# A decoder trunk on one core: down's weights on GpSimd's queue, another cut of the seven-product groups, another opening and a shorter final norm

## The chip, the cores and the metric

The kernel runs on one NeuronCore of a Trainium2 chip. The core has TensorE (PE, matrix products; its weight loads are listed apart as PEld), VectorE (DVE), ScalarE (ACT), GpSimd (POOL) and SyncE (SP), which run side by side and wait for one another through semaphores. Data comes from HBM by DMA; a DMA is issued in order on the queue of one engine, and all queues are served by the same 16 DMA engines. The metric is the device time of one execution in microseconds (us). Time before: 1836.87 us, the median of three runs (1836.17 to 1838.67).

## The reference

The input x is 512 tokens by 1024 features in float32. Two layers follow one another; layer 0 has a gated linear attention (GLA) as its mixer and layer 1 a stick-breaking attention (SB). Each layer is

```
x = x + 0.5 * swiglu(rmsnorm(x, ffn1_norm[i]), gate, up, down)
h = rmsnorm(x, mix_norm[i]);  x = x + mixer_i(h)
x = x + 0.5 * swiglu(rmsnorm(x, ffn2_norm[i]), gate, up, down)
```

with `swiglu(h) = (silu(h @ w_gate) * (h @ w_up)) @ w_down`, `rmsnorm(x, g) = x * rsqrt(mean(x*x) + 1e-6) * g`, w_gate and w_up of 1024 x 2816 and w_down of 2816 x 1024. A final rmsnorm with `final_norm` gives the output. The four FFNs hold most of the arithmetic, and the change is in them, in the first microseconds ahead of them and in the final norm.

## The kernel before

**Arithmetic.** Every product is float32 by three passes. A matrix a is cut in two fp32r parts: ScalarE casts it (h, line L126), VectorE subtracts (l = a - h, L127), and TensorE adds h·h, l·h and h·l. The two lines stand in `Entry.split`; the tiles are wh and wl, four buffers of each. The activations are kept the same way (xh/xl, nh/nl, th/tl, hh/hl) with features on the 128 partitions and the 512 tokens along the free dimension.

**The feed.** All weight work is a list of entries in `Feed`. An entry has units (a chunk of weights in HBM, a view of it, its size) and a body, which issues the products. When entry i starts, `Feed.start` (L142) looks ahead: it cuts the next entries' units, as far as the four wh/wl buffers go, builds the views (sums) of the next four, and issues the loads of the next six. `Chunk.load` (L91) issues a load on SyncE's queue, into the tag raw (gate, up, mixers: 1 MB, two buffers) or the tag rawd (down: 512 KB, two buffers of their own). A load waits on the queue until its buffer is free, and what stands behind it waits too. Each queue and each engine works strictly in order.

**Seven-product groups.** Most gate and up weights, and a part of down's, are multiplied by a Strassen-Winograd scheme: a tile is seen as four quarters A11, A12, A21, A22, and seven products of quarter size replace eight. For gate and up this is `FFN.seven` (L665 to L771): two entries per group. The first has as units A11 together with A12 (one cut of 128 x 1024, name ax) and the sums s12 (L677, L678 on VectorE); its four products go to the PSUM tiles ps_w, ps_q, ps_w and ps_z, and ScalarE copies ps_w to ps_z (L718) after the first. The second has the sums s34 (L683, L684) and A22 (128 x 512), with three products; L704 and L707 then apply silu or the gate and put the result together. A product is 12 matmuls (L694) of 128 x 256. For down it is `seven_down` (L333 to L427): the same scheme on two rawd chunks (lower and upper), with sums at L353 to L361, matmuls at L369, additions to x at L375, and the two copies of ps_w to ps_z at L387, which TensorE needs before it writes ps_w again in the third product. Down's other groups are plain (`down`, addition at L324). Within an FFN of six groups, the second and the fourth group's down is by seven products.

**The opening** (`begin`, L1495 to L1690) is written out by hand and pinned in order: loads of x and of the first gate (eg) and up (eu) weights in halves (L1527), 32 transposes of x (`turn`, L1574), scaling into xh and xl (`scale`), cuts of the first weights (L1544, L1546), 48 products (L1599) in the order gate 0-1, transposes, gate 2-3, up 0-1, transposes, up 2-3, the norm's factor R (L1665), and 24 products more. The feed's own products follow (L66).

**The end** (`to_tokens`, L1441; `last`, L1458). The last FFN's down products give tokens by features. fin, the final norm's gains on all partitions, is loaded on GpSimd's queue (L1445). For each of four token tiles: x is added up (L1462), ScalarE squares it with a sum (L1471), `rstd_1` (L494) turns the two sums into the factor r in six steps on VectorE and ScalarE (an addition, a square root, a reciprocal, and three steps that refine it), x and xf are scaled (L1478, L1480), and both leave on SyncE's queue (L1479, L1481). The last tile's second half comes in two pieces of 256 columns.

## Time and profile before

| what | value |
|---|---|
| median of three runs | 1836.87 us |
| profiled execution | 1839.01 us |
| its span, first to last instruction | 1837.2 us |
| mean granted TensorE clock | 0.998 |
| TensorE busy | 1821.0 us (99%), 12476 matmuls |
| VectorE busy | 1530.1 us (83%) |
| ScalarE busy | 1068.4 us (58%) |
| GpSimd busy | 8.7 us, 20 instructions |
| DMA by SyncE's queue | 176.18 MB, 30.2% of the 16 engines' time |
| DMA by GpSimd's queue | 1.05 MB |
| last output issued | 1833.91 us |

The profile is of one execution. Starts are microseconds from its first instruction. A row of a timeline gives start, duration, engine, line, operation and tiles, and in brackets how long the engine had been idle before it and what released it. A row of the waits gives who waited for whom, the total, how many times, and the longest. The granted clock is that of TensorE as a share of full speed. PEld overlaps PE. A queue is written as SPq, ACTq or POOLq.

### The profile page before, as it was taken

Reading aid. Unit: us, or ns where it says so; the run is one execution under the profiler, and the core shown is the slowest. Engines: PE = TensorE matmul, PEld = TensorE weight load, DVE = VectorE, ACT = ScalarE, POOL = GpSimd, SP = SyncE. Lnnn points to the kernel's source line nnn. Section 1 sums busy time; section 2 is a strip of 40 time slices with the busy share of each in tenths; the row PEclk is TensorE's granted clock in tenths of the full one; section 3 lists DMA queues with packets and bytes.
Section 4 is the critical chain, followed back from the end, with each engine's and each line's share of the span. In section 5 each row is a group of like instructions: output and inputs, shape, how many; then the busy total and the mean of one; then the engine's idle time right before and its main releaser. Section 6 shows DMA issues by size and latency. Waiting matters only on the chain. (4 is left out here: it accounts for less than half of the span.)

```text
span 1837.2 us, 30777 instructions
## 1 busy us (share of the span) xinstructions
PE 1821.0 (99%) x12476; PEld 1657.2 (90%) x12476; DVE 1530.1 (83%) x2509; ACT 1068.4 (58%) x1842; POOL 8.7 (0%) x20
## 2 busy tenths in 40 slices
PE   8999999999999999999999999999999999999998
PEld 7999999889888899999889999998888788999997
DVE  8999797776787989888798988976878769898885
ACT  6556565444555556555565555645878855565554
POOL 0000000100000000000000000000000000000000
PEclk9999999999999999999999999999999999999999
DMA  5333324221223232323233232322221222333331
GB/s 161 118 124 116 103 93 139 79 69 49 68 69 115 92 111 97 127 93 115 75 121 107 91 125 92 119 86 85 70 70 58 69 92 92 115 106 113 104 104 69
DMA packets 177649, 179.20 MB, mean 98 GB/s; under 512 B 4130, under 2 KB 168020, under 8 KB 177508
## 3 DMA queue, kind: packets, MB, share of 16 engines
q1 hardware_dynamic: 176800, 176.18, 30.2%
q8 instruction: 97, 1.59, 0.4%
q0 software_dynamic: 608, 1.05, 0.2%
q14 instruction: 44, 0.36, 0.1%
q10 hardware_dynamic: 100, 0.03, 0.0%
HBM read 175.17 MB, written 2.10 MB: 96 GB/s over the span
## 5 line engine op out<-in xcount | busy, mean ns | idle before, releaser
L127 DVE TENSOR_TENSOR wl<-raw,wh 128x1024 fp32r<-128x1024 f32 x242 | 256.0, 1061 | 88.0 <-ACT wh L126 46.6
L126 ACT CAST wh<-raw 128x1024 fp32r<-128x1024 f32 (+1 forms) x242 | 223.0, 922 | 157.4 <-PE ps_f L66 35.7
L127 DVE TENSOR_TENSOR wl<-s,wh 128x1024 fp32r<-128x1024 f32 x176 | 214.0, 1219 | 40.4 <-PE ps_z L694 38.5
L694 PE MATMUL ps_w<-th,wh 128*128 128x256 f32 x864 | 239.0, 277 | 0.3
L694 PE MATMUL ps_w<-tl,wh 128*128 128x256 f32 x864 | 238.7, 276 | 0.0
L694 PE MATMUL ps_w<-th,wl 128*128 128x256 f32 x864 | 238.7, 276 | 0.0
L126 ACT CAST wh<-s 128x1024 fp32r<-128x1024 f32 x176 | 184.9, 1050 | 82.8 <-DVE s L684 27.7
L66 PE MATMUL ps_f<-xh,wh 128*128 128x512 f32 x432 | 172.5, 399 | 0.0
L66 PE MATMUL ps_f<-xl,wh 128*128 128x512 f32 x432 | 169.3, 392 | 0.0
L66 PE MATMUL ps_f<-xh,wl 128*128 128x512 f32 x432 | 168.9, 391 | 0.0
L694 PEld LDWEIGHTS ps_w<-th,wh 128*128 128x128 f32 x864 | 162.2, 188 | 0.9 <-ACT ps_z L718 0.9
L694 PEld LDWEIGHTS ps_w<-th,wl 128*128 128x128 f32 x864 | 162.4, 188 | 0.0
L66 PE MATMUL ps_d<-hh,wl 128*128 128x512 f32 x416 | 162.2, 390 | 0.0
L66 PE MATMUL ps_d<-hh,wh 128*128 128x512 f32 x416 | 162.2, 390 | 0.0
L694 PEld LDWEIGHTS ps_w<-tl,wh 128*128 128x128 f32 x864 | 162.2, 188 | 0.0
L66 PE MATMUL ps_d<-hl,wh 128*128 128x512 f32 x416 | 161.8, 389 | 0.0
L126 ACT CAST wh<-rawd 128x1024 fp32r<-128x1024 f32 (+1 forms) x84 | 81.5, 971 | 96.7 <-PE ps_d L66 45.0
L127 DVE TENSOR_TENSOR wl<-rawd,wh 128x1024 fp32r<-128x1024 f32 (+1 forms) x84 | 93.2, 1118 | 20.7 <-PE ps_z L694 11.5
L324 DVE SCALAR_TENSOR_TENSOR x<-ps_d,x 128x512 f32<-128x512 f32 x120 | 80.9, 686 | 21.4 <-PE ps_d L66 21.0
L66 PEld LDWEIGHTS ps_f<-xl,wh 128*128 128x128 f32 x432 | 81.1, 188 | 17.3
L66 PEld LDWEIGHTS ps_f<-xh,wl 128*128 128x128 f32 x432 | 81.3, 188 | 15.6
L66 PEld LDWEIGHTS ps_f<-xh,wh 128*128 128x128 f32 x432 | 81.3, 188 | 15.4
(348 smaller groups left out, 5279.8 us busy)
## 6 DMA issues: line engine op xcount, KB each, us to landing
raw<-in_ffn_w_gate_dram SPq DMA_DIRECT2D x43, 1024.0 KB, 5.3
raw<-in_ffn_w_up_dram SPq DMA_DIRECT2D x43, 1024.0 KB, 5.7
rawd<-in_ffn_w_down_dram SPq DMA_DIRECT2D x84, 512.0 KB, 3.6
raw<-in_gla_w_in_dram SPq DMA_DIRECT2D x12, 1024.0 KB, 5.4
raw<-in_sb_w_in_dram SPq DMA_DIRECT2D x16, 512.0 KB, 3.8
raw<-in_gla_w_out_dram SPq DMA_DIRECT2D x4, 1024.0 KB, 5.0
raw<-in_sb_w_in_dram SPq DMA_DIRECT2D x4, 1024.0 KB, 5.2
raw<-in_sb_w_out_dram SPq DMA_DIRECT2D x4, 1024.0 KB, 5.0
```

Of the source, the lines that this page charges most:

```text
L66: st["pe"] = nc.tensor.matmul(ps, l, r, start=first, stop=last).ins
L126: st["cut"] = nc.scalar.copy(h, r).ins
L127: nc.vector.tensor_tensor(out=l, in0=r, in1=h.bitcast(F32), op=ALU.subtract)
L324: nc.vector.scalar_tensor_tensor(out=xs[k], in0=ps, scalar=0.5, in1=xs[k], op0=ALU.mult, op1=ALU.add)
L694: st["pe"] = nc.tensor.matmul(o, l_, r_, start=first and j + n == 0, stop=j == 3 and n == 2, skip_group_check=True).ins
```

## The change

**Loads.** A chunk of down's weights is loaded through GpSimd's queue instead of SyncE's. The buffers stay as they are, two of tag rawd.

**Seven-product groups.** The first entry of a group has three units: A11 alone (512 columns), the sums s12, and a2, which is A12 together with A22 (1024). The second entry has only s34; its last product takes A22 from a2. `Entry.split` can cut a unit that comes in two pieces, since down's A12 and A22 lie in two tiles: such a unit is two casts and two subtractions of 512. For gate and up the number and sizes of the cuts are the same as before; for down, 16 cuts of 1024 columns become 32 of 512. The products themselves and their order are the same.

**Opening.** The up weights' first half is loaded before the second half of x. Ten matmuls of the ones tile by itself, 128 columns each, whose result is overwritten, are put among the first transposes (six ahead, one each before the third and the fourth tile's, two behind). The first 24 products, gate 0-3 and up 0-3, follow one another, and all 16 transposes of the second half of x come behind them; the scalings and cuts on ScalarE and VectorE are reordered to suit.

**Final norm.** fin is scaled once by a constant on VectorE. `rstd_1` adds the second sum inside the square root's instruction, and refines with one division less: r = 1/(y + v/y). In the last tile the last square is taken on VectorE, x is scaled and sent in two halves of 256 columns, and xf leaves on ScalarE's queue.

The diff, cut to its core:

```diff
@@ -88,7 +88,7 @@
                     self.t = st["few"].tile([P, self.n, self.m], F32, tag="rawd", bufs=2, name="rawd")
                 else:
                     self.t = wp.tile([P, self.n, self.m], F32, tag="raw", bufs=2, name="raw")
-                nc.sync.dma_start(self.t, self.src)
+                (nc.gpsimd if self.few else nc.sync).dma_start(self.t, self.src)
...
-                    st["cut"] = nc.scalar.copy(h, r).ins
-                    nc.vector.tensor_tensor(out=l, in0=r, in1=h.bitcast(F32), op=ALU.subtract)
+                    pieces = r if isinstance(r, tuple) else (r,)
+                    for i, part in enumerate(pieces):
+                        k = slice(i * n // len(pieces), (i + 1) * n // len(pieces))
+                        st["cut"] = nc.scalar.copy(h[:, k], part).ins
+                        nc.vector.tensor_tensor(out=l[:, k], in0=part, in1=h[:, k].bitcast(F32), op=ALU.subtract)
...
-        feed.q.append(
-            Entry([(lower, lambda t: t, 4, 256), (lower, sums_12, 4, 256)], body_1, NEAR, feed.q[-1].place != NEAR)
-        )
+        units = [(lower, lambda t: halves()[0], 2, 256), (lower, sums_12, 4, 256), (lower, lambda t: halves()[1::2], 4, 256)]
+        feed.q.append(Entry(units, body_1, NEAR, feed.q[-1].place != NEAR))
         assert not feed.q[-1].lead
-        feed.q.append(Entry([(lower, sums_34, 4, 256), (upper, lambda t: halves()[3], 2, 256)], body_2, NEAR))
+        feed.q.append(Entry([(lower, sums_34, 4, 256)], body_2, NEAR))
...
@@ -493,17 +495,14 @@
     def rstd_1(sums, more):
 
-        v = sp.tile([P, 1], F32, tag="rv", bufs=2, name="rv")
-        nc.vector.tensor_scalar(out=v, in0=sums, scalar1=more, scalar2=D * EPS, op0=ALU.add, op1=ALU.add)
         y = sp.tile([P, 1], F32, tag="ry", bufs=2, name="ry")
-        nc.scalar.activation(y, v, AF.Sqrt)
-        nc.vector.reciprocal(y, y)
-        q = sp.tile([P, 1], F32, tag="rq", bufs=2, name="rq")
-        nc.vector.scalar_tensor_tensor(out=q, in0=y, scalar=v, in1=y, op0=ALU.mult, op1=ALU.mult)
-        c = float(D) ** 0.5
-        nc.vector.tensor_scalar(out=q, in0=q, scalar1=-0.5 * c, scalar2=1.5 * c, op0=ALU.mult, op1=ALU.add)
+        nc.scalar.activation(y, sums, AF.Sqrt, bias=more)
+        v = sp.tile([P, 1], F32, tag="rq", bufs=2, name="rv")
+        nc.vector.tensor_tensor(out=v, in0=sums, in1=more, op=ALU.add)
         r = sp.tile([P, 1], F32, tag="r4", bufs=2, name="r1")
-        nc.vector.tensor_tensor(out=r, in0=y, in1=q, op=ALU.mult)
+        nc.vector.reciprocal(r, y)
+        nc.vector.scalar_tensor_tensor(out=v, in0=r, scalar=v, in1=y, op0=ALU.mult, op1=ALU.add)
+        nc.vector.reciprocal(r, v)
         return r
...
-                prod(w, a22, 0, lambda j: self.t_half(3, j), first=False)
+                prod(w, v["a2"], 0, lambda j: self.t_half(3, j), first=False, c0=P)
...
-            entry = Entry([(ch, lambda t: t[:, :, 0:P], KD, P), (ch, sums_12, KD, P)], body_1, NEAR, lead)
+
+            units = [(ch, lambda t: t[:, 0:4, 0:P], 4, P), (ch, sums_12, KD, P), (ch, lambda t: t[:, 4:8], 4, 256)]
+            entry = Entry(units, body_1, NEAR, lead)
             feed.q.append(entry)
-            feed.q.append(Entry([(ch, sums_34, KD, P), (ch, lambda t: t[:, 4:8, P:], 4, P)], body_2, NEAR))
+            feed.q.append(Entry([(ch, sums_34, KD, P)], body_2, NEAR))
...
+        nc.vector.tensor_scalar(out=fin, in0=fin, scalar1=2.0 * float(D) ** 0.5, scalar2=None, op0=ALU.mult)
...
@@ -1460,25 +1464,34 @@
         x, fin = xt[i, dh], st["fin"]
         c = slice(c0, c1)
         nc.vector.scalar_tensor_tensor(out=x[:, c], in0=ps, scalar=0.5, in1=x[:, c], op0=ALU.mult, op1=ALU.add)
-        if c0 == 0:
-            n = 2 * i + dh
+        end = c0 > 0
+        n = 2 * NT if end else 2 * i + dh
+        sq = st["sq"][:, n : n + 1]
+        if end:
+            junk = sp.tile([P, T], F32, tag="ss", name="junk")
+            nc.vector.scalar_tensor_tensor(
+                out=junk[:, 0 : c1 - c0], in0=x[:, c], scalar=1.0, in1=x[:, c], op0=ALU.mult, op1=ALU.mult, accum_out=sq
+            )
         else:
-
-            n = 2 * NT
-            s = st["sq"][:, n - 2 : n - 1]
-            nc.vector.tensor_tensor(out=s, in0=s, in1=st["sq"][:, n - 1 : n], op=ALU.add)
-        sq = st["sq"][:, n : n + 1]
-        nc.scalar.activation(ps, x[:, c], AF.Square, accum_out=sq)
+            nc.scalar.activation(ps, x[:, c], AF.Square, accum_out=sq)
         if dh == 0:
             st["xf"] = st["tp"].tile([P, T], F32, tag="s", bufs=4, name="xf")
             nc.vector.tensor_tensor(out=st["xf"], in0=x, in1=fin[:, 0:T], op=ALU.mult)
-        elif c1 == T:
+            st["sum"] = sp.tile([P, 1], F32, tag="rv", bufs=2, name="sum")
+            nc.vector.tensor_scalar(out=st["sum"], in0=sq, scalar1=D * EPS, scalar2=None, op0=ALU.add)
+        elif c1 < T:
+            nc.vector.tensor_tensor(out=st["sum"], in0=st["sum"], in1=sq, op=ALU.add)
+        else:
             rows = out[0, i * P : (i + 1) * P]
-            r = rstd_1(sq, st["sq"][:, 2 * i : 2 * i + 1])
-            nc.vector.scalar_tensor_tensor(out=x, in0=x, scalar=r, in1=fin[:, T:D], op0=ALU.mult, op1=ALU.mult)
-            nc.sync.dma_start(rows[:, T:D], x)
+            r = rstd_1(sq, st["sum"])
+
+            for a0, a1 in ((0, T // 2), (T // 2, T)) if end else ((0, T),):
+                nc.vector.scalar_tensor_tensor(
+                    out=x[:, a0:a1], in0=x[:, a0:a1], scalar=r, in1=fin[:, T + a0 : T + a1], op0=ALU.mult, op1=ALU.mult
+                )
+                nc.sync.dma_start(rows[:, T + a0 : T + a1], x[:, a0:a1])
             nc.scalar.activation(st["xf"], st["xf"], AF.Copy, scale=r)
-            nc.sync.dma_start(rows[:, 0:T], st["xf"])
+            (nc.scalar if end else nc.sync).dma_start(rows[:, 0:T], st["xf"])
...
-        load_x(0), load_w(eg, 0), load_x(1), load_w(eu, 0), load_w(eg, 1), load_w(eu, 1)
+        load_x(0), load_w(eg, 0), load_w(eu, 0), load_x(1), load_w(eg, 1), load_w(eu, 1)
...
+        for k in range(4):
+            pst[k] = psum("ps_x")
+        g, u = psum("ps_f"), psum("ps_f")
+
+        def busy(n):
+
+            for _ in range(n):
+                pin(nc.tensor.matmul(u[:, 0:P], ones, ones, start=True, stop=True))
+
+        busy(6)
         for i in range(NT):
             if i == 3:
                 pin(nc.tensor.transpose(psg[:, 0:16], gls[0], ident[0:16, 0:16]))
+            if i >= 2:
+                busy(1)
             for k in range(4):
                 turn(k, i)
+        busy(2)
         square(0, 0, True), square(1, 0, False), square(2, 0, True)
         pin(nc.vector.tensor_copy(gT[:, 0:16], psg[:, 0:16]))
         square(3, 0, False)
-        g, u = psum("ps_f"), psum("ps_f")
         scale(0)()
         cut(eg, 0)()
+        scale(1)(), scale(2)(), scale(3)()
+        cut(eu, 0)()
+        keep(0), keep(1)
         square(0, 1, True), square(1, 1, False)
-        scale(1)(), scale(2)()
         square(2, 1, True), square(3, 1, False)
-        low = scale(3)
...
-        low()
-        low = cut(eu, 0)
         st["sqrt"] = pin(nc.scalar.activation(y, v, AF.Sqrt)).ins
-        keep(0), keep(1), keep(2)
-        low()
+        keep(2)
...
-        products(eg, g, (0, 1))
-        for k in (4, 5):
+        products(eg, g, range(4))
+        products(eu, u, range(4))
+        for k in range(4, KD):
             for i in range(NT):
                 turn(k, i)
-        products(eg, g, (2, 3))
-        products(eu, u, (0, 1))
-        for k in (6, 7):
-            for i in range(NT):
-                turn(k, i)
-        products(eu, u, (2, 3))
```

More of the change, by code (lines that the diff above doesn't have):

```diff
@@ L362, in sums_34, with prod @@
             return s
-        def prod(ps, w, k0, step, m, b, first):
+        def prod(ps, w, k0, m, b, first):
             for c in range(2):
                 bh, bl = hs[c][b]
-                wh, wl = (t[:, k0 + step * c, m * P : (m + 1) * P] for t in w)
+                wh, wl = (t[:, k0 + c, m * P : (m + 1) * P] for t in w)
                 for n, (l_, r_) in enumerate(((wh, bh), (wl, bh), (wh, bl))):
@@ L377, in body_1 @@
         def body_1(W):
-            ax, s = W
+            a11, s, v["a2"] = W
             ws, zs, qs = [], [], []
@@ L381, in body_1 @@
                 ws.append(psum("ps_w")[:, 0:H])
-                prod(ws[m], ax, 0, 2, m, "b11", True)
+                prod(ws[m], a11, 0, m, "b11", True)
             for m in range(2):
@@ L394, in body_1 @@
             for m in range(2):
-                prod(ws[m], s, 2, 1, m, "t2", False)
+                prod(ws[m], s, 2, m, "t2", False)
                 add(m, 0, 1, ws[m])
@@ L398, in body_1 @@
             for m in range(2):
-                prod(zs[m], ax, 1, 2, m, "b21", False)
+                prod(zs[m], v["a2"], 0, m, "b21", False)
                 add(m, 0, 0, zs[m])
@@ L404, in body_2 @@
         def body_2(W):
-            s, a22 = W
+            (s,) = W
             ws, qs = v["w"], v["q"]
@@ L409, in body_2 @@
             for m in range(2):
-                prod(ws[m], s, 0, 1, m, "t3", False)
+                prod(ws[m], s, 0, m, "t3", False)
                 nc.scalar.copy(u3[:, m], ws[m])
@@ L414, in body_2 @@
             for m in range(2):
-                prod(qs[m], s, 2, 1, m, "b22", False)
+                prod(qs[m], s, 2, m, "b22", False)
                 add(m, 0, 1, qs[m])
@@ L685, in sums_34, with prod @@
                 return s
-            def prod(o, w, w0, b, first=True, lead=None):
+            def prod(o, w, w0, b, first=True, lead=None, c0=0):
                 for j in range(4):
                     bh, bl = b(j)
-                    wh, wl = w[0][:, w0 + j], w[1][:, w0 + j]
+                    wh, wl = (t[:, w0 + j, c0 : c0 + P] for t in w)
                     for n, (l_, r_) in enumerate(((wh, bh), (wl, bh), (wh, bl))):
@@ L709, in body_1 @@
             def body_1(W):
-                ax, s = W
+                a11, s, a2 = W
+                v["a2"] = a2
                 v["w"], v["q"] = psum("ps_w"), psum("ps_q")
@@ L716, in body_1 @@
                 o0, o1 = v["o"] = [self.tp.tile([P, T], F32, tag="t", name=n) for n in ("o0", "o1")]
-                prod(w, ax, 0, half(0, 0), lead=entry.first if lead else None)
+                prod(w, a11, 0, half(0, 0), lead=entry.first if lead else None)
                 nc.scalar.copy(z, w)
@@ L725, in body_1 @@
                 yield
-                prod(z, ax, 4, half(4, 0), first=False)
+                prod(z, a2, 0, half(4, 0), first=False)
                 gate(o0, 0, z)
@@ L730, in body_2 @@
             def body_2(W):
-                s, a22 = W
+                (s,) = W
                 w, q = (v[n][:, 0:H] for n in "wq")
```

4 lines of the change are left out of this document (2 added, 2 removed).

## The prediction

> **What bounds the kernel now.** I read the page's busy shares first, then the waits of TensorE and of VectorE, then the timelines of DMA issue, VectorE and TensorE around TensorE's longest wait, and last the opening and the tail.
>
> ```profile
> PE 1821.0 (99%) x12476; PEld 1657.2 (90%) x12476; DVE 1530.1 (83%) x2509; ACT 1068.4 (58%) x1842; POOL 8.7 (0%) x20
> PE ps_x L1574 <- DMA x<-in_x_dram: 4.2, 2, 3.7
> PE ps_q L369 <- DVE o L707: 1.4, 1, 1.4
> PE ps_w L369 <- ACT ps_z L387: 1.2, 2, 0.7
> DVE s L677 <- DMA raw<-in_ffn_w_up_dram: 5.0, 5, 2.4
> SPq L91 <- DVE wl L127: 1578.6, 184, 28.0
> ```
>
> TensorE is the bound: 1821.0 of 1837.2 us, and of its waits outside the opening and the tail these rows are the large ones, 2.6 us together. The diff adds no product and takes none away, so all it can change is the start, the end, and that little in between. The last row is why a queue matters: SyncE's queue spends 1578.6 us waiting for rawd and raw buffers to come free, in order.
>
> Around the longest wait (start, duration, instruction; idle time before it and releaser in brackets):
>
> ```profile
> 844.53 0.37 SPq L91 DMA_DIRECT2D rawd<-in_ffn_w_down_dram  x1
> 845.30 0.37 SPq L91 DMA_DIRECT2D raw<-in_ffn_w_up_dram  x1
> 853.45 0.69 DVE L677 TENSOR_TENSOR s<-raw 128x512 f32<-128x512 f32 x1 [2.41 <-DMA raw<-in_ffn_w_up_dram]
> 855.54 0.38 PE L369 MATMUL ps_q<-hh,wh 128*128 128x256 f32 x1 [1.43 <-DVE o L707]
> 857.00:861.00 4.00, 4.00 (x24) 4.00 (x23) 3.22 (x9) 1.24 (x2) 0.00 (x0) 0.58 0.76 261
> ```
>
> raw (1 MB) is issued behind rawd (512 KB) and lands 8 us later, so the sums at L677 start late, the additions at L707 queued behind them are late, and TensorE stands for 1.43 us. The last row (four microseconds after; the 0.58 is the granted clock, then DMA share and GB/s) shows the second price: 0.58 over 4.00 us is 3.4 us at half clock, a loss of 0.42 x 4.00 = 1.7 us. So this one late load costs 1.43 + 1.7 = 3.1 us.
>
> TensorE's two waits for ps_z have the same origin:
>
> ```profile
> 743.93 0.69 DVE L677 TENSOR_TENSOR s<-raw 128x512 f32<-128x512 f32 x1 [1.86 <-DMA raw<-in_ffn_w_gate_dram]
> 746.10 0.64 ACT L387 COPY ps_z<-ps_w 128x256 f32<-128x256 f32 x2
> 746.53 0.39 PE L369 MATMUL ps_w<-hh,wh 128*128 128x256 f32 x1 [0.55 <-ACT ps_z L387]
> 1040.59 0.69 DVE L677 TENSOR_TENSOR s<-raw 128x512 f32<-128x512 f32 x1 [1.24 <-DMA raw<-in_ffn_w_up_dram]
> ```
>
> VectorE waits for raw, ScalarE's copies at L387 come late behind VectorE's sums, TensorE waits 0.55 us, and 0.7 at the second place.
>
> **The change, part by part.** Rows for the prices:
>
> ```profile
> 853.26 0.28 PE L369 MATMUL ps_q<-hh,wh 128*128 128x256 f32 x1
> 853.83 0.28 PE L369 MATMUL ps_q<-hl,wh 128*128 128x256 f32 x1
> L126 ACT CAST wh<-rawd x84: 604/1053/1058, 42.3 to 1788.6; 128x1024 fp32r<-128x1024 f32 x68, 128x512 fp32r<-128x512 f32 x16
> L127 DVE TENSOR_TENSOR wl<-rawd,wh x84: 681/1218/1227, 53.2 to 1789.7; 128x1024 fp32r<-128x1024 f32 x68, 128x512 fp32r<-128x512 f32 x16
> 1773.76 0.53 POOL L1445 DMA_DIRECT2D fin<-in_final_norm_dram  x1 [545.23 <-DVE wl L127]
> fin<-in_final_norm_dram POOLq DMA_DIRECT2D x1, 512.0 KB, 3.7
> rawd<-in_ffn_w_down_dram SPq DMA_DIRECT2D x84, 512.0 KB, 3.6
> 1773.00:1780.00 7.00, 7.00 (x41) 6.08 (x40) 7.00 (x14) 1.67 (x2) 0.53 (x1) 1.00 0.43 131
> ```
>
> Five matmuls take 0.57 us, so a product of 12 takes 12 x 0.114 = 1.37 us and a seven-product group 9.6.
>
> *Splitting A11 and A12+A22.* A raw tile is now done with once a2 is cut, which the group's fourth product needs; before, A22 held it to the seventh. That gives the next raw load about four products, 4 x 1.37 = 5.5 us, more; and it no longer waits behind a rawd issue. The largest wait of VectorE for raw was 2.41 us, under 5.5. All three stalls go: -1.43 - 0.55 - 0.7 - 1.7 (clock) = -4.4. What is late next is ps_z, below. Sixteen 1024-casts of rawd become 32 of 512: 16 x (2 x 0.61 - 1.05) = 2.7 us more on ScalarE, 16 x (2 x 0.69 - 1.22) = 2.6 on VectorE; both lie beside TensorE, VectorE having 1837 - 1530 = 307 us free. Without that cover they would be 2.6 us of path.
>
> *Down's weights on GpSimd's queue.* SyncE's queue loses 84 issues with their waits, and a raw load is held up by its own buffer alone. The 84 issues at 0.53 each are 45 us on an engine busy for 8.7; free. On that queue gr, tri, w, lf (ahead of the first mixer) and negm (in the second) now stand between the FFNs' rawd loads, and fin behind the last one: a load of gr that waits for TensorE would hold the next FFN's first rawd, whose cut is only needed a mixer later, so I price it at nothing; if that cover were gone it would be one landing, 3.7. The nearest row for the landing is fin, also 512 KB: 3.7 us against 3.6, hence no price per load; bounds 3.6 and, from a load queued behind another, 3.6 + 3.7 = 7.3. There is one kind of tight place, eight of them, one after every second seven-product down group: ScalarE casts a rawd tile (1024 columns) just ahead of the two ps_z copies, and that tile loads only once the A12+A22 cuts of the previous one are through. From those cuts to the copies' use there are six products, 6 x 1.37 = 8.2 us; the chain is two casts and subtractions of 512 (0.61 + 2 x 0.69 = 2.0, with hand-overs about 2.3), 3.7 landing, 1.05 cast, 0.64 copies: 7.7 to 8.0. Margin 0.2 to 0.5 us. I take 0.1 a place, +0.8; bounds 0 and 8 x 1.0 (landing 5 us).
>
> [...]
>
> In this case's rows: over 1773 to 1780 VectorE was busy 7.00 of 7.00 us, fin's load was issued at 1773.76 in the midst of it, and landed in 3.7.
>
> *The new fin scaling* on VectorE, 128x1024, about 1.2 us, waits for fin's landing. fin waits, as before, for an s buffer (released in before by 1773.76); some eight microseconds of VectorE work lie between that release and the scaling, landing 3.7: 0, or up to +1.2 if the x addition queued behind it is needed.
>
> *The opening.*
>
> ```profile
> 1.01 0.29 POOL masks.py:199 TENSOR_SCALAR_AFFINE_SELECT ident<-ident 128x128 f32<-128x128 f32 x1
> 3.25 0.38 SPq L1525 DMA_DIRECT2D raw<-in_ffn_w_gate_dram  x1
> 15.71 4.02 SPq L91 DMA_DIRECT2D rawd<-in_ffn_w_down_dram  x2
> 6.00:8.00 2.00, 2.00 (x11) 1.62 (x10) 0.46 (x2) 0.78 (x3) 0.00 (x0) 1.00 0.99 347
> 9.19 0.80 PE L1599 MATMUL ps_f<-xh,wh 128*128 128x512 f32 x1 [0.64 <-ACT wh L1544]
> 11.51 0.63 PE L1599 MATMUL ps_f<-xh,wl 128*128 128x512 f32 x1
> 11.94 0.63 PE L1599 MATMUL ps_f<-xl,wh 128*128 128x512 f32 x1
> 14.66 0.39 PE L1599 MATMUL ps_f<-xh,wh 128*128 128x512 f32 x1
> 14.89 0.40 PE L1599 MATMUL ps_f<-xh,wl 128*128 128x512 f32 x1
> 16.72 1.03 PE L1574 MATMUL ps_x<-ident,x 128*128 128x128 f32 x8
> 18.98 1.05 PE L1665 MATMUL ps_R<-dg,gT 128*128 128x128 f32 x8
> 25.62 0.50 PE L66 MATMUL ps_f<-xh,wh 128*128 128x512 f32 x1
> ```
>
> The first two rawd loads were issued at 15.71 because SyncE had everything else to issue first. On GpSimd they have nothing ahead but the identity (1.01 + 0.29): 1.05 MB enters at 1.3 us DMA engines that run full (0.99, 347 GB/s), worth 1.05 / 0.347 = 3.0 us of them, while the first x tiles and the first gate weights are what TensorE waits for. The first product (9.19) moves by 0 to +3.0; I take 1.8, since x's tiles (from 0.74) are partly ahead: 11.0. From there the 48 products no longer have transposes between the first 24. At half clock a 512 matmul takes 11.94 - 11.51 = 0.43 us, at full 14.89 - 14.66 = 0.23. If the clock rises at the same 13.8 us, 2.8 us hold 6.5 products, the other 41.5 take 9.5, the 16 transposes 2 x 0.8 and R 0.8 (1.03 and 1.05 in the rows, whose last 0.2 the next matmul overlaps), the last small transpose before the feed 0.3: 13.8 + 12.2 = 26.0 against 25.62, +0.4; with VectorE's later chain I take +0.5.
>
> The ten new ones-matmuls are to bring the full clock sooner. The granted clock in before rose only after products from 9.19, not with the transposes. [...]
>
> *The final norm.* The last tile's steps in before:
>
> ```profile
> 1830.83 0.39 ACT L1471 ACTIVATE ps_bt<-x 128x256 f32<-128x256 f32 x1 [0.23 <-DVE gT L1469]
> 1831.37 0.21 DVE L497 TENSOR_SCALAR rv<-gT 128x1 f32<-128x1 f32 x1 [0.57 <-ACT ps_bt L1471]
> 1832.69 0.75 DVE L1478 SCALAR_TENSOR_TENSOR x<-x,r,fin 128x512 f32<-128x512 f32 x1
> 1833.48 0.33 SPq L1481 DMA_DIRECT2D out_dram<-xf  x1
> 1833.91 0.38 SPq L1479 DMA_DIRECT2D out_dram<-x  x1
> ```
>
> The square goes to VectorE right behind the addition (ends about 1831.15 instead of 1831.34), the square root needs no addition ahead (-0.25), and the chain after it is two steps shorter (-0.2 each): r near 1832.1. The xf output leaves on ScalarE's queue, x in two halves: last issue about 1833.05 instead of 1833.91: -0.9; bounds -1.2 and +0.3 (three outputs instead of two).
>
> Sum: -4.4 + 0.8 + 0.5 - 0.9 = -4.0. The profiled execution took 1839.01 (span 1837.2 and 1.8 around it), 2.1 above the median of 1836.87; I count from the median: 1832.9.
>
> **The rivals.**
> Warm early: the ones-matmuls bring the full clock before the first product; 6.5 to 8 matmuls save 0.2 each, -1.7: 1831.2. For it: TensorE gets work ahead of 3.71. Against: transposes at 3.7 to 8.5 gave no clock.
> [...]
> Doesn't do what it says: raw still lands late (the same 16 DMA engines carry it, now with rawd at its side): no -4.4: 1837.3. Against: 5.5 us more.
> Slower: GpSimd's loads land at 5 us instead of 3.7; each of the eight tight places stalls 0.9 to 1.0, +7 in place of 0.8, and the longest of them take the clock down at 1.7 each: 1839 to 1843. It decides from about 1.05 us a place, landing above 5.1. The row against it is fin's 3.7; only one row of that size.
>
> **How the numbers follow.** 0.2% is 3.7 us, about what a measurement of this kernel can tell from no change: faster is below 1833.2, slower above 1840.5. Forecast 0.50 (its own range 1831 to 1836; 0.29 of it below 1833.2), warm early 0.14, opening late 0.14, doesn't do 0.07, slower 0.15 (0.02 of it under 1840.5). Faster 0.29 + 0.14 = 0.43; same 0.21 + 0.14 + 0.07 + 0.02 = 0.44; slower 0.13. The range goes from the better end of warm early (1829.5) to the near end of the slower case (1839.5).
>
> **What would show it.** Right: no VectorE wait at L676 for raw, clock full from 861 back to 850, no TensorE wait over 1 us between 30 and 1825; TensorE's first product near 11, first matmul of the feed near 26; last output issued near 1833 less what was gained. Wrong: rawd landings over 5 us from GpSimd's queue, ScalarE waiting for rawd ahead of the ps_z copies, or half clock after 14 us.

## The result and the profile after

The changed kernel takes 1842.85 us, the median of seven runs (1842.44 to 1844.4), against 1836.87 for the kernel before (median of seven, 1835.39 to 1840.0). The ratio is 1.0033, 95% interval 1.0023 to 1.0042: slower by 6.0 us, where 4.0 us faster was forecast. The profiled execution took 1842.67, with a span of 1840.9, 3.7 longer than the span before. (The execution profiled before lay 2.1 above its own median, so 3.7 in the spans and 6.0 in the medians go together.)

From the page of the changed kernel, the busy times and the DMA issues, and TensorE's larger waits:

```profile
PE 1826.8 (99%) x12496; PEld 1662.0 (90%) x12496; DVE 1544.7 (84%) x2529; ACT 1059.3 (58%) x1856; POOL 71.6 (4%) x104
rawd<-in_ffn_w_down_dram POOLq DMA_DIRECT2D x84, 512.0 KB, 4.0
PE ps_x L1587 <- DMA x<-in_x_dram: 2.4, 1, 2.4
PE ps_q L372 <- DVE o L706: 1.1, 4, 0.3
PE ps_w L693 <- ACT u L736: 0.9, 2, 0.7
```

The large waits of before in the middle are gone: TensorE's 1.4 us for o and its two for ps_z no longer stand in the list, nor does VectorE wait for raw anywhere. In their place stand four waits of 0.3 for o and two for u. TensorE is busy 5.8 us longer, though only the ten ones-matmuls were added (20 instructions of 128 columns in the trace), most of them in time that was idle before: other matmuls took longer.

To find where the time came in, I matched the same matmul in both traces and took the difference of its starts (after less before):

| where, by the time before | after - before, us | change in the stretch |
|---|---|---|
| first matmul of the feed (25.62) | +4.04 | +4.04 |
| 713 | +7.13 | +3.1 |
| 1063 | +0.93 | -6.2 |
| 1814 to 1830 | +4.10 | +3.2 |
| end of the span | +3.7 | -0.4 |

The gain that was forecast is there, between 713 and 1063. The opening takes most of it, and two other stretches give back 6.3 us.

**The opening.** GpSimd's issue, two windows (busy time and count of PE, PEld, DVE, ACT and POOL, then granted clock, DMA share, GB/s), and from the timelines of the changed kernel TensorE's transposes, ScalarE's cast of the first gate weights and TensorE's products:

```profile
1.44 1.63 POOL L91 DMA_DIRECT2D rawd<-in_ffn_w_down_dram  x2
6.00:8.00 2.00, 0.33 (x2) 0.33 (x3) 0.00 (x0) 0.35 (x1) 0.00 (x0) 0.89 0.99 357
8.00:10.00 2.00, 1.96 (x8) 1.30 (x7) 0.42 (x2) 0.37 (x2) 0.00 (x0) 0.50 1.10 322
3.75 1.32 PE L1587 MATMUL ps_x<-ident,x 128*128 128x128 f32 x8
7.67 1.12 PE L1587 MATMUL ps_x<-ident,x 128*128 128x128 f32 x4 [2.38 <-DMA x<-in_x_dram]
12.00 0.62 ACT L1557 CAST wh<-raw 128x512 fp32r<-128x512 f32 x1 [1.03 <-DMA raw<-in_ffn_w_gate_dram]
12.67 0.79 PE L1612 MATMUL ps_f<-xh,wh 128*128 128x512 f32 x1 [0.93 <-ACT wh L1557]
17.83 0.39 PE L1612 MATMUL ps_f<-xl,wh 128*128 128x512 f32 x1
29.64 0.73 PE L66 MATMUL ps_f<-xh,wh 128*128 128x512 f32 x2
```

The two rawd loads enter at 1.44 and the DMA engines run full (0.99 and 1.10 in the two windows). Two things follow. First, the full clock does not last. Behind the ones-matmuls and the first transposes it is there from 4.2: matmuls of 128 columns start every 0.11 us then, every 0.21 until then, and the eight transposes from 3.75 take 1.32 us, the four from 7.67 already 1.12. But x's third tile is late, TensorE idles 2.38 us for it, and the granted clock stands at 0.50 from 7.6 to 17.8, where a matmul of 512 columns starts every 0.43 us, and every 0.23 from there on. In before the same two paces meet at 13.8; the windows print 1.00 ahead of that, as they do ahead of 4.2 here, but the pace is that of the 0.50. Second, the first gate weights are late. Their first half, issued at 3.24, lands at 11.98, where it landed at 7.52 before; ScalarE waits 1.03 us for it, so the first product starts at 12.67 (9.19 before).

**The middle.** The window of before's half clock; VectorE and TensorE around the first of the four waits for o; ScalarE and TensorE around the longer wait for u:

```profile
857.00:861.00 4.00, 3.95 (x33) 3.62 (x32) 3.19 (x5) 2.73 (x6) 0.00 (x0) 1.00 0.64 242
257.16 0.68 DVE L130 TENSOR_TENSOR wl<-rawd,wh 128x512 fp32r<-128x512 f32 x1
257.76 0.68 DVE L677 TENSOR_TENSOR s<-s,raw 128x512 f32<-128x512 f32 x1
259.96 1.22 DVE L130 TENSOR_TENSOR wl<-s,wh 128x1024 fp32r<-128x1024 f32 x1
261.69 0.42 DVE L706 TENSOR_TENSOR o<-ps_w,o 128x256 f32<-128x256 f32 x1
262.17 0.38 PE L372 MATMUL ps_q<-hh,wh 128*128 128x256 f32 x1 [0.29 <-DVE o L706]
668.52 1.05 ACT L129 CAST wh<-s 128x1024 fp32r<-128x1024 f32 x1 [1.59 <-DVE s L677]
669.47 0.37 ACT L736 COPY u<-ps_w 128x256 f32<-128x256 f32 x1
669.89 0.38 PE L693 MATMUL ps_w<-th,wh 128*128 128x256 f32 x1 [0.67 <-ACT u L736]
```

The clock is full at 857. But VectorE works without a gap from 254.4 to 262.1, and the second subtraction of down's A12+A22, which is now cut in two pieces (257.16), the sum of the next group (257.76) and its cut (259.96) stand ahead of the last addition at L706 (261.69). That addition ends at 262.1 and releases TensorE, whose next matmul starts 0.57 us after the one before it where 0.11 is the rule. A wait of 0.28 to 0.29 stands once in each of the four FFNs (262.2, 713.4, 1163.4 and 1624.7). At 668.52 ScalarE's cut of the next sums, itself waiting for VectorE, stands ahead of the copy of u that frees ps_w: 0.67. None of the two stood in the trace before.

**A slower rhythm.** The other part of the give-back is in no list of waits. Two stretches of the changed kernel, TensorE's groups by line (count, busy us, mean ns of one), first 140 to 162 us, then 165 to 189:

```profile
L693 PE MATMUL ps_w<-th,wh 128*128 128x256 f32 x16 | 4.4, 276 | 0.0
...
L693 PE MATMUL ps_w<-th,wh 128*128 128x256 f32 x20 | 5.6, 281 | 0.0
```

The same matmul with no idle time takes 276 ns in one stretch and 281 in the other, and the distance from start to start is 113 ns in the first and 118 in the second, at the full granted clock (1.00 in both). The slow stretch begins at a matmul that came late behind a semaphore by too little to be listed (163.12) and lasts, with one break near 183, to the wider matmuls at 190. I call such a stretch a spell. A matmul takes 117.8 ns in it instead of 113.3, so 3.8% of its length is lost. Counted as all distances of 117 to 119 ns, spells make up 61 us of the profiled execution before and 123 us after: 3 and 44 us up to 713, 19 and 1 between 713 and 1063, 38 and 78 from there on. In the two stretches that give back, that is 80 x 0.038 = 3.0 us; with the waits for o (four times 0.46 above the usual distance) and for u (0.67 and 0.24) it makes 5.8 of the 6.3 us. Of the 6.2 us gained between them, 18 x 0.038 = 0.7 is spells, and no term of the forecast.

How far this belongs to the change is open, since spells differ from execution to execution. By the same count the second profile of the kernel before holds 85 us of them; over all runs, the profiles with the whole new split hold 82 to 313 us (the one with added wide matmuls, below, left aside), those with the old split 24 to 177.

**The tail.** TensorE's last matmul and the last issues:

```profile
1834.09 0.28 PE L66 MATMUL ps_bt<-wh,hl 128*128 128x256 f32 x1
1836.83 0.81 SPq L1492 DMA_DIRECT2D out_dram<-x  x2
1837.07 0.38 ACTq L1494 DMA_DIRECT2D out_dram<-xf  x1
```

The last output issue comes 3.15 us after the last matmul's start, against 3.91 before, but the end only 6.8 instead of 7.2.

### The profile page after: what moved, and what is told of

The parts are those of the page before. It is cut to its first block, busy times and chain, and to the rows that moved or that the text cites. A ratio compares the mean times of both kernels' runs of the same rounds, so it can differ in the third digit from the quotient of the medians.

```text
span 1840.9 us, 30850 instructions
## 1 busy us (share of the span) xinstructions
PE 1826.8 (99%) x12496; PEld 1662.0 (90%) x12496; DVE 1544.7 (84%) x2529; ACT 1059.3 (58%) x1856; POOL 71.6 (4%) x104
## 4 chain that ended last, share of the span: by engine, by line
PE 83%; issue 10%; DVE 4%; DMA 2%; ACT 1%; POOL 0%; DVEq 0%; POOLq 0%; ACTq 0%; SPq 0%
PE ps_f L66 18%; PE ps_w L693 17%; PE ps_d L66 14%; PE ps_q L693 8%; PE ps_t L66 5%; PE ps_z L693 4%; PE ps_b L66 4%; PE ps_w L372 4%; PE ps_q L372 2%; PE ps_S L66 1%; PE ps_z L1319 1%; PE ps_oT L1381 1%; DVE wl L130 1%; PE ps_z L372 1%; PE ps_bt L66 1%
## 5 line engine op out<-in xcount | busy, mean ns | idle before, releaser
L130 DVE TENSOR_TENSOR wl<-raw,wh 128x512 fp32r<-128x512 f32 (+1 forms) x242 | 256.7, 1061 | 66.6 <-ACT wh L129 47.6
L129 ACT CAST wh<-raw 128x512 fp32r<-128x512 f32 (+1 forms) x242 | 223.4, 924 | 97.9 <-PE ps_f L66 32.9
L91 POOL DMA_DIRECT2D rawd<-in_ffn_w_down_dram x84 | 62.9, 750 | 1692.9 <-DVE wl L130 1109.3
```

The source lines that it names most:

```text
L91: (nc.gpsimd if self.few else nc.sync).dma_start(self.t, self.src)
L129: st["cut"] = nc.scalar.copy(h[:, k], part).ins
L130: nc.vector.tensor_tensor(out=l[:, k], in0=part, in1=h[:, k].bitcast(F32), op=ALU.subtract)
```

## The experiments

Each is compared with runs of the kernel before on the same chip, whose median is given. None leaves out or changes anything that reaches the output; the ones-matmuls that two of them drop are overwritten anyway.

**The first two down loads back on SyncE's queue, at their old place; all else as changed.**

```diff
-                (nc.gpsimd if self.few else nc.sync).dma_start(self.t, self.src)
+                st["rawd"] = st.get("rawd", 0) + self.few
+                (nc.gpsimd if self.few and st["rawd"] > 2 else nc.sync).dma_start(self.t, self.src)
```

> The changed kernel, but the first two loads of down's weights go out on SyncE's queue behind all of the opening's loads, as in before; the other 82 stay on GpSimd's. Theory (their 1.05 MB in the first microseconds holds back x and the first gate weights): first product near 9.3 instead of 12.67, the feed's first matmul between 25 and 26.2 instead of 29.64, total about 1839 (3.5 to 4.5 less than the changed kernel). Rival (the new order of the opening and its ones-matmuls cost it): feed's first matmul stays above 28.5, total about 1842.

1837.7 against 1837.11, ratio 1.0004 (0.9994 to 1.0014): two DMAs out of 84 are worth 5.2 us of the 6.0. Its opening:

```profile
9.26 0.49 PE L1613 MATMUL ps_f<-xh,wh 128*128 128x512 f32 x1 [0.51 <-ACT wh L1558]
24.34 0.73 PE L66 MATMUL ps_f<-xh,wh 128*128 128x512 f32 x2
```

The feed starts at 24.34 instead of 29.64, 5.3 us earlier, which is what the medians say. Its runs spread over 8.5 us (1834.94 to 1843.45). The profiled one was the slowest, and it held 313 us of spells; (313 - 123) x 0.038 = 7.2 us more than the changed kernel's, which is how an opening 5.3 shorter can end 0.8 later. The edit moves the two loads to another queue and to a later time at once; whether they would cost anything if issued late on GpSimd's queue, no run shows.

**Without the ones-matmuls** (the changed kernel, ten matmuls dropped).

```diff
             for _ in range(n):
-                pin(nc.tensor.matmul(u[:, 0:P], ones, ones, start=True, stop=True))
+                pass
```

> The changed kernel without the ten ones-matmuls (their result is overwritten, nothing computed is lost). If the early loads of down's weights alone hold up the opening, and the ones-matmuls are lost to the wait for x that follows them: first product and feed's first matmul within 0.3 us of the changed kernel's 12.67 and 29.64, total 1842.5 to 1843. If the ones-matmuls themselves do harm (they stand ahead of the transposes): feed's first matmul 1 to 2 us earlier, total 1841 to 1842. If they help even here: later.

1842.48 against 1837.34, 1.0027 (1.0017 to 1.0038): as slow as with them. In its profile the feed starts at 28.40, 1.2 earlier than with them. They neither cause the late opening nor help against it: the full clock that the changed kernel's profile shows behind them from 4.2 on is half again at 7.6.

**The opening of before, and the first two loads on SyncE.** The first edit, and all of `begin` as before.

> The changed kernel with the opening of before and its first two loads of down's weights on SyncE's queue: what is left is queue, split and norm. Both theories: feed's first matmul near 25.6. If the middle of the kernel is a wash (stalls at late raw loads gone, others in their place) and the tail gains 0.4: 1836 to 1837. If the middle gains the 4.4 us that I forecast: 1832 to 1833. Against the run without the first two loads on GpSimd it prices the new opening by itself: theory 0 to -1, rival +3.

1841.47 against 1837.11, 1.0023 (1.0014 to 1.0031). Split, norm and 82 loads on GpSimd cost 4.4 without the new opening, and 0.6 with it (the first experiment). In its profile the feed starts at 26.42, against 24.34 there: 2.1 of the difference of 3.8 is in the opening. Another 1.3 is a wait for ps_z that the first experiment's profile does not have:

```profile
858.43 1.05 ACT L130 CAST wh<-rawd 128x1024 fp32r<-128x1024 f32 x1 [2.58 <-DMA rawd<-in_ffn_w_down_dram]
859.80 0.39 PE L373 MATMUL ps_w<-hh,wh 128*128 128x256 f32 x1 [1.31 <-ACT ps_z L391]
```

This is the tight place that the prediction worked out. The rawd load was issued on GpSimd's queue at 852.96 and landed at 858.35, 5.4 us later; ScalarE's cast of it stands ahead of the two ps_z copies. In the run without the ones-matmuls TensorE waits 0.54 us there (860.50); in the changed kernel ScalarE waits 1.12 us for rawd (859.23) and TensorE not at all.

**The new opening alone, on the kernel before.**

> Before with the new opening alone; all of down's weights on SyncE's queue. Theory: feed's first matmul between 25 and 26.2 (before 25.62), total within 1 us of before. Rival: feed's first matmul above 28.5, total 3 to 4 above before, 1840 to 1841.

1837.06 against 1837.11, 1.0003 (0.9994 to 1.0012): nothing in the medians, though its feed starts at 23.65, 2.0 before the 25.62 of the profile before. TensorE's waits show where the gain went:

```profile
PE ps_w L369 <- ACT ps_z L387: 2.5, 2, 1.3
PE ps_q L369 <- DVE o L707: 1.7, 2, 1.4
```

With the smaller ones its waits for ps_z and o in the FFNs come to 4.8 us, against 2.7 before, and VectorE waits 15.7 us for raw against 12.5. With the earlier start more of the raw loads come late.

**The 82 later down loads on GpSimd's queue, alone, on the kernel before.** The first edit in before's line L91; the instructions of TensorE, ScalarE and VectorE and their order are before's.

> Before with the 82 later loads of down's weights on GpSimd's queue, nothing else changed. Theory (raw no longer queues behind rawd): VectorE's waits for raw fall from 12.5 us to under 5, the stall after raw's late landing is gone, total 1 to 4 below before: 1833 to 1836. Rival (GpSimd's landing of 4.0 us instead of 3.6 makes new waits for rawd): waits of ScalarE for rawd of 5 to 10 us, TensorE's waits not less, total 0 to 2 above before.

1855.68 against 1837.11, 1.0101 (1.0086 to 1.0115): 18.6 us slower, the largest effect of any one part. VectorE's and TensorE's waits, the two issues ahead of one of the stalls, the sum that waits, and two microseconds of DMA between them (window columns as above):

```profile
DVE s L678 <- DMA raw<-in_ffn_w_up_dram: 16.9, 12, 2.7
PE ps_q L370 <- DVE o L708: 4.4, 4, 2.0
251.25 0.75 POOL L92 DMA_DIRECT2D rawd<-in_ffn_w_down_dram  x1 [23.13 <-DVE wl L128]
251.59 0.37 SPq L92 DMA_DIRECT2D raw<-in_ffn_w_up_dram  x1
260.36 0.69 DVE L678 TENSOR_TENSOR s<-raw 128x512 f32<-128x512 f32 x1 [2.67 <-DMA raw<-in_ffn_w_up_dram]
254.00:256.00 2.00, 2.00 (x20) 2.00 (x19) 1.43 (x3) 1.68 (x2) 0.00 (x0) 1.00 1.00 367
```

The two loads, released by the same buffers as before, are now issued 0.34 us apart on two queues and are in flight side by side. rawd lands 5.7 us after its issue and raw 8.7; the same two took 3.6 and 5.9 before. In the window rawd gets 0.51 MB in 127 packets and raw 0.23 in 221.

The trace's issues and landings show the same over the whole run. After the opening, 30 raw loads of gate and up have a rawd load in flight beside them and take 7.2 us in the median, the 43 others 5.3; rawd takes 5.7 beside a raw load and 4.0 alone. In the kernel before, where both share SyncE's queue, 34 such raw loads take 5.9. VectorE's waits for raw grow from 5.0 to 16.9 us (up weights), and TensorE's waits for o, ps_z and u from 2.6 us to 12.3, of which the row shows 4.4. The 9.7 us more are about half of the 21 between the two profiled spans; the rest I have not traced. The other queue is no free road: side by side both transfers took longer than in the kernel before (raw 7.2 against 5.9, rawd 5.7 against 3.6), and raw was the urgent one.

**The split alone, on the kernel before** (all loads on SyncE's queue).

> Before with the new split of the seven-product groups alone; all loads on SyncE's queue, old opening, old norm. Theory (the split changes VectorE's order, so that the gating at L706 and L737 stands behind cuts and sums): TensorE's four waits of 0.3 for the gated o, one in each FFN, and its wait for u at 669 are there, and the waits for late raw loads are gone or not: total 1836 to 1839. Rival (GpSimd's landing of 4.0 us makes these waits): they are gone, total 1832 to 1835.

1838.68 against 1837.34, 1.0011 (1.0001 to 1.002): slower by 1.3. TensorE's waits, and two matmuls of its opening, which is before's:

```profile
PE ps_q L372 <- DVE o L709: 1.1, 4, 0.3
PE ps_w L696 <- ACT u L739: 0.9, 2, 0.7
8.75 0.50 PE L1604 MATMUL ps_f<-xh,wh 128*128 128x512 f32 x1 [0.95 <-ACT wh L1549]
9.97 0.39 PE L1604 MATMUL ps_f<-xl,wh 128*128 128x512 f32 x1
```

VectorE waits for raw no more and the stalls of before are gone; but the four waits for o and the two for u are here, so they come from the split and not from the queue. Spells last 188 us in its profile. And the old opening, without any ones-matmul, ran at full pace from the first product (0.39 at 9.97, where the profile before has 0.63): when the full clock begins differs from one execution to another. In the four other profiles of the old opening on record the granted clock rises at 13.8 to 15.7 us and the feed starts at 25.6 to 26.4. In all eight profiles of the new opening without the early loads the clock rises at 4.7 to 7.4, and the feed starts at 23.7 to 24.3.

**All of the change but the queue** (changed kernel, every down load on SyncE), and **the opening and the norm alone, on the kernel before.**

> The changed kernel with all loads of down's weights on SyncE's queue: opening, split and norm stay. Opening as in the run without the two early loads (first product near 9.3, feed near 24.3). If the queue is a gain once groups are split (raw no longer behind rawd): slower than that run's 1837.7, 1838 to 1840. If the queue costs by its landing: 1833 to 1836.

> Before with the new opening and the new final norm, old groups, old queue. Opening -1.7 and tail -0.4 in the profile's terms: last output issued 0.4 to 0.9 sooner after the last matmul than in before (3.9 us); total 1834.5 to 1836.5, if the middle stays as in before.

The first: 1834.83 against 1837.34, 0.999 (0.9981 to 0.9998), 2.5 us faster than before and the best of all. The second: 1835.62, 0.999 (0.9982 to 0.9999). The two can't be told apart, so the split, which alone lost 1.3, gains nothing that can be measured on top. TensorE's waits show why, first with the split, then without:

```profile
PE ps_w L693 <- ACT u L736: 1.3, 2, 0.7
PE ps_q L372 <- DVE o L706: 1.1, 4, 0.3
```

```profile
PE ps_q L369 <- DVE o L704: 2.4, 2, 1.2
PE ps_q L369 <- ACT o L701: 0.9, 1, 0.9
PE ps_w L369 <- ACT ps_z L387: 0.7, 1, 0.7
```

2.4 us against 4.0: one set of waits for another. And with 141 us of spells against 24, the split's profiled execution loses 4.4 us there, though both counts differ much from run to run. Against the first experiment, the 82 later loads on GpSimd cost 1837.7 - 1834.83 = 2.9 us (the two ratios' intervals make that some 0.2 to 5): far less than the 18.6 above. With the split in place no VectorE wait for raw is left in either, and few raw loads meet a rawd load any more: 4 of 73 in the first experiment, where the queue alone had 30 of 73. What is left is rawd's own landing, 3.9 us in the median against 3.5 on SyncE's queue, and ScalarE's waits for it: 5.0 to 13.3 us in the four profiles with split and queue, 2.1 in the one without the queue.

**The same, without the ones-matmuls.**

> The changed kernel with all loads of down's weights on SyncE's queue and without the ten ones-matmuls. If these bring the clock up where no early load of down's weights is in the way: without them the first products run at half clock until 12 to 14 us, feed's first matmul 25.5 to 26.5 instead of about 24.3, total 1.2 to 2 above the 1834.8 with them. If the transposes would do it by themselves: no change.

1835.93 against 1836.85, 0.9992 (0.9982 to 1.0001), not to be told from the version with them. Full pace from the first product, with only the transposes ahead of it (the four from 7.07 take 0.79 us where the profile before has 1.11, and the first product 0.49 against 0.80):

```profile
8.81 0.49 PE L1612 MATMUL ps_f<-xh,wh 128*128 128x512 f32 x1 [0.95 <-ACT wh L1557]
```

**The split for gate and up only, and for down only** (all loads on SyncE; `seven_down`, or `FFN.seven`, as before).

> The changed kernel with all loads of down's weights on SyncE's queue and down's groups split as in before; gate and up keep the new split. If TensorE's four waits of 0.3 us for the gated o (one in each FFN) come from down's cuts in two pieces on VectorE: they are gone here, total 1832.5 to 1834.5. If they come from the gate and up groups' new order: they stay, total 1834 to 1836. The wait for u, 0.7 at 663 in before's time, comes by the trace from a cut of s12 queued ahead of u on ScalarE in a gate group: it stays.

> The counterpart: the new split for down's groups alone, gate and up as in before, all loads on SyncE's queue, new opening and norm. Late raw loads come back (VectorE waits over 10 us for raw, stalls of TensorE at down's groups), since gate and up hold their raw tile to the seventh product again: total 1835.5 to 1838. If the four waits for the gated o come from down's pieces they are here.

1851.85 and 1918.66 against 1836.85: 1.0075 (1.0062 to 1.0089) and 1.0447 (1.043 to 1.0464). TensorE's waits, gate and up first:

```profile
PE ps_w L694 <- ACT wh L129: 5.7, 8, 0.7
```

```profile
PE ps_w L372 <- ACT wh L129: 43.9, 16, 4.1
```

TensorE waits for cuts themselves. In the second the mean granted clock is 0.981, and 75 us at half clock make up some 38 of its 82. A group of before has two cuts in each of its entries, a new one three and one; with both kinds in one FFN the four wh/wl buffers, as I read it, no longer come round in step. The split works only as a whole, and these two say nothing on the four waits for o, since the order on VectorE is another: which of the pieces and sums makes these waits stays open.

**The kernel before, profiled again.**

> The kernel before, unchanged, profiled a second time, to see which of its stalls come again. If late raw loads are a matter of chance in each execution: VectorE's waits for raw again near 12 us, but the long stall of TensorE at another place than 854 or absent, the two waits for ps_z at other places. If they are fixed by the order of work: 1.4 us at 854 again, with half clock after it.

1838.34. The stall at 854 and the window after it:

```profile
855.80 0.39 PE L369 MATMUL ps_q<-hh,wh 128*128 128x256 f32 x1 [1.46 <-DVE o L707]
857.00:861.00 4.00, 4.00 (x35) 3.99 (x35) 4.00 (x9) 2.41 (x5) 0.00 (x0) 1.00 0.72 249
```

The same stall, 1.46 us, but no half clock behind it; the two waits for ps_z come again too, at 746.8 and 1042.3. So both profiles of this kernel have the stalls, and only one of them the 1.7 us that half clock cost. The timed runs of the kernel before that stand beside these experiments say the same: of 79, 71 have a mean granted clock of 0.999 or 1.000, and 8 have 0.997 or 0.998, as the first profiled execution has.

**One matmul of 512 columns ahead of each of the 72 gate and up groups** (on the version with all loads on SyncE), to see whether a wide matmul ends a spell; its result is overwritten.

```diff
+                nc.tensor.matmul(v["q"], a11[0][:, 0], st["h"][0], start=True, stop=True)
```

> The changed kernel with all loads of down's weights on SyncE's queue, and one extra matmul of 128x512, whose result is overwritten, ahead of each of the 72 gate and up groups by seven products. In the profiles of all kernels with the new split there are spells of 18 to 48 us in which a 128x256 matmul takes 118 ns from start to start instead of 113. If such a spell is a lead of the weight loads that TensorE lost in a short wait, and that a wide matmul gives back: no spell longer than a group (9.6 us) here, total 72 x 0.23 = 16.4 above 1834.8 less up to 5. If it is something of the clock: spells of 18 us and more as before.

1866.71 against 1835.91, one run each. Windows between wide matmuls and one group of each, the slow stretch first:

```profile
119.50:128.60 9.10, 9.10 (x79) 9.10 (x78) 9.10 (x15) 4.78 (x10) 0.00 (x0) 1.00 0.09 25
129.60:148.20 18.60, 18.60 (x166) 18.60 (x165) 18.28 (x33) 10.99 (x21) 0.00 (x0) 1.00 0.27 88
...
L693 PE MATMUL ps_w<-th,wh 128*128 128x256 f32 x10 | 2.8, 281 | 0.0
...
L693 PE MATMUL ps_w<-th,wh 128*128 128x256 f32 x12 | 3.3, 276 | 0.0
```

Of the 78 stretches with at least 40 distances between two wide matmuls, 73 have one rhythm throughout, 113 or 118 ns; the other five change it at an interruption inside. And 46 of the 78 came out slow; spells make up 511 us. The wide matmuls cost 72 x 0.23 = 16.6, the extra spells (511 - 141) x 0.038 = 14.1, together 30.7; between the two profiled executions there are 1866.71 - 1837.13 = 29.6. So a wide matmul did not bring the fast rhythm back here; the rhythm behind it was either.

## Why the prediction was wrong

The sum was -4.0; the medians give +6.0. Term by term:

- **Opening, taken at +0.5: +4.0 in the trace. This is the step that failed most.** The sum took 1.8 of the 3.0 us of bytes, on the ground that x's tiles are partly ahead, and the clock at the old 13.8. The first product moved by 3.5, more than all the bytes, and the full clock came 4.0 later (17.8). A late opening was given 0.14; how long half clock would last behind one, no row of before showed, and in the run it lasted 10.2 us. What the step missed: the two loads hold back the first gate weights by 4.5 us, which sets the first product, and x's third tile by 1.6, for which TensorE idles 2.38 us; the clock, full from 4.2 on, is half behind that wait. That the wait took it down is my reading: of the two waits of 1.43 and 1.46 us at 854 only one has half clock behind it. The first experiment shows that it is these two loads: 5.2 us in the medians, and without them the new opening is ahead of the old.
- **The three stalls, -4.4: right in the place and the cause, too large in the size.** VectorE's waits for raw are gone in every version with the split. But 1.7 of it was half clock of one execution, which the second profile of before does not have, and the mean clock is that low in one timed run of ten; 2.7 belongs in a forecast of the median.
- **What is late next, ps_z, +0.8: right as a mechanism, but not what the changed kernel's profile shows.** ps_z is not in its list of waits; at the place worked out, TensorE waits 1.31 and 0.54 us in two of the three other profiles with split and queue. The chain's own terms give 7.4 to 7.7 us, not 7.7 to 8.0, so the margin was 0.5 to 0.8; what uses it up is a landing of 4.4 to 5.4 us there where 3.7 was taken.
- **The cuts in pieces, taken at nothing: wrong.** The step that failed is "both lie beside TensorE, VectorE having 1837 - 1530 = 307 us free": free time in sum says nothing of the order. By the order in the trace, pieces, sums and cuts stand ahead of additions and copies that TensorE needs next. The waits for o and u are 2.7 us, and the run with the split alone has them too.
- **The slower rhythm** had no term in the sum. In the two profiles it is (123 - 61) x 0.038 = 2.4 us, but since spells vary by execution, this can't be laid to the change.
- **No price per load on GpSimd's queue: wrong.** The nearest row, fin's 3.7, was a single load. rawd's landing is 4.0 in the median, with VectorE busy 84% of the span, ScalarE waits 9.5 us for it in all, and the 82 loads cost 2.9 us in the medians. That the queue leaves raw "held up by its own buffer alone" is true of its issue, not of its landing (in the run with the queue alone 7.2 us beside a rawd load, 5.3 without). The rival "Slower" named this term, at over twice its size (+7); it needed eight stalls of 0.9 to 1.0, and no profile with split and queue has more than one of that size; "Doesn't do what it says" (raw still late, with rawd at its side) is what happens where raw has no slack, 18.6 us in the run with the queue alone.
- **The tail, -0.9: -0.4.** The steps went nearly as worked out (last issue 0.76 earlier), but half of it did not reach the end.
- **Warm early:** right for the versions with the two loads out of the opening (full clock by 7.4 us in all eight profiles), but also without ones-matmuls, and in before's own opening once in five. In the medians the new opening alone gains nothing, since VectorE's later waits for raw take it back (15.7 us against 12.5); with the new norm it gains 1.7.

The parts by medians: the two early loads +5.2, the other 82 some +2.9, the split -0.8 (not to be told from nothing) to +1.3, the opening with the norm -1.7. They depend on each other (the run with the old opening shows 3.8 for the new one), so the sum is a rough one. Open is what decides between 113 and 118 ns, and whether the split makes more of the slow ones.

## What to carry to other kernels

GpSimd's idle queue issued the first two rawd loads at 1.44 us, where SyncE's had come to them at 15.71, and that cost 5.2 us here: before moving loads to an idle queue, ask which transfers are then in flight, and which of the two is urgent; the first loads of the program above all, since they meet the opening. When work is cut finer on an engine that has time to spare, look at what stands behind each new piece in that engine's order, not at its sum of free time (307 us of VectorE here, and 2.7 us of waits for o and u all the same). A half clock (3.4 us in one of two profiles here), a start of the full clock (before 8.75 or at 13.8 us with the same opening) or a rhythm (61 or 85 us of spells in the kernel before) seen in one profile may be that execution's; profile the kernel before twice before such a term goes into a sum.

## What the runs showed of the hardware that was not expected

- Back-to-back fp32r matmuls of 128x256 ran at one of two steady distances, 113 or 118 ns, at a granted clock of 1.00 in both. In the changed kernel's profile the slow one came in rows of up to 226 matmuls (from 1064.8), and one row began at a matmul that was late by too little to be listed (163.12). In the run with wide matmuls 73 of 78 stretches between two of them kept one distance throughout, and five changed it at an interruption inside. The slow distance held for 24 to 511 us of an execution, 3.8% of which was lost.
- Two queues in flight did not share the DMA engines evenly: GpSimd's got 0.51 MB against 0.23 in 2 us (254 to 256 in the run with the queue alone), with packets of 4.0 KB against 1 KB. In the run with the queue alone GpSimd's first packet of a rawd load came 1.5 us after the issue in the median (0.7 to 3.3), SyncE's of a raw load 1.0.
- A wait of 1.43 us was followed by 3.4 us at half clock in one execution, and one of 1.46 at the same place by none in another; the wait of 2.38 in the changed kernel's opening was followed by 10.2. The first product ran at full pace in one execution of before's opening (8.75) and at half until 13.8 in another.
